# Wide gate and up products, padded values, pair matrices in turn and the inversion first, in a three-network block chain on one core

## The chip, the core and the metric

One Trainium2 chip, one of its cores. The metric is the device time of one execution in microseconds (us). TensorE is called PE here, VectorE DVE, ScalarE ACT, GpSimd POOL and SyncE SP (it issues the DMAs).

## The reference

A first block (layer 1) and a second block of two layers (layer 2, called 0 and 1) work on 256 tokens with 1024 features, and a last norm ends the program. Each layer is a mixer, whose parts are put side by side and projected back to 1024, and a feed-forward network with 2816 hidden units. All in single precision.

```python
# layer 1
h = rms_norm(x, pre_mix_norm)
mix = concat(rg_lru(h), gla_chunked(h), moba_attention(h))   # moba: 8 heads of 64 features
x = x + rms_norm(mix @ w_out, post_mix_norm)
h = rms_norm(x, pre_ffn_norm)
f = (silu(h @ w_ffn_gate) * (h @ w_ffn_up)) @ w_ffn_down
x = x + rms_norm(f, post_ffn_norm)
# layer 2, twice
h = rms_norm_2(x, attn_norm_g)
ya = rwkv7_mixer(...)      # recurrent: 4 heads of 64
yb = dilated_mixer(...)    # attention: 4 heads of 64
yc = mla_mixer(...)        # latent attention: 4 heads, values of 128
x = x + concat(ya, yb, yc) @ w_out
h = rms_norm_2(x, ffn_norm_g)
x = x + (silu(h @ ffn_w_gate) * (h @ ffn_w_up)) @ ffn_w_down

# the recurrent step of rwkv7_mixer
sa = einsum('bhvk,bhk->bhv', state, kk_t)
state = state * w_t - sa[..., None] * b_t + v_t[..., None] * k_t
y = einsum('bhvk,bhk->bhv', state, r_t)
```

## The kernel before

**Split products.** Every weight is read once from HBM as a raw tile of 128 x 1024 (`wraw`, three buffers). ACT rounds it into a high part `whi` (L279), and DVE, for a few POOL (L281, L283), subtracts to get the low part `wlo`. The activations are split likewise: `hT[0]` (tile `hTh`) and `hT[1]` (`hTl`), features on partitions, 256 tokens wide. A product is the sum of three: high by high, high weight by low activation, low weight by high activation. `fm` does that with the weight stationary and the 256 tokens moving (L431 to L433), `tm` with the tokens stationary and 512 weight columns moving (L442 to L445), `mm3` for single pieces (L313 to L315).

**Feed-forward networks** (`ffn`). The 2816 hidden units are 22 blocks of 128; the first two go through `tm`, the other twenty through the loop over f. In it, a block's gate and up products are put side by side into the two halves of one PSUM bank, taken in turn from two pairs, `p` and `r` (48 matmuls 256 wide); ACT takes silu of the gate half (L583), DVE multiplies by the up half (L584), the product `sl` is split into `hd` high and low (ACT L586, DVE L587), and one block later PE multiplies `hd` by the down weights (L313 to L315, twelve matmuls 512 wide) into four banks that stay accumulating.

**Attention** (`attention`, `softmax_head`). For each head: scores into a bank `s`, softmax on DVE and ACT, three transposes of 128 x 128 on PE (L464), and the values' product in two matmuls (L467, L468), which PE does in two passes each as its operands are full single precision. Two heads of 64 features share a bank `o`: one writes its upper 64 rows, the other its lower 64.

**The recurrent mixer** (`recurrent`, generators `c`, `i`, `v`, `o`, `u`) turns the recurrence into blocks of 128 tokens. `pairs` multiplies the decayed keys of one head by `n.AR` (64 features deep, so 64 rows of PE) and copies the masked result from a bank to a zeroed tile: LN in bank `r`, MN in bank `p`, four heads each. `solve` inverts triangular matrices: it starts from the 32 x 32 diagonal blocks, which POOL copies out of LN into `Nd` (L1200), and doubles them in four rounds. A round is a matmul batch `Xd` by LN, a copy `v1` on ACT (L986), a batch `v1` by `Zd` (L976), a masked copy on DVE (L991) and a transpose on DVE (L992, the first one L980); each batch comes in two halves of 16 matmuls 32 x 32. Then the blocks are put together in pairs up to 128 (L1003 and behind).

**Order.** Code is written as generators, and a string (`PLAN1`, `PLAN2`) says in which order their pieces are laid down. A scheduler then orders each engine's instructions by when it takes them to be ready and by priority, which is the order of laying down where nothing else is said. Each engine works in order. PSUM has two banks `p`, two `r`, two `s`, one `t`, one `o`.

## Time and profile before

| | |
|---|---|
| runs | 1023.39, 1024.9 and 1031.35 us, median 1024.9 |
| the profiled execution | 1030.67 us, span 1028.9 us |
| PE busy | 988.9 us (96%) |
| DVE busy | 610.5 us (59%) |
| ACT busy | 515.1 us (50%) |
| POOL busy | 86.2 us (8%) |
| layer 1's mixer | 0 to about 132 us |
| feed-forward, steady | 147 to 324, 497 to 670, 846 to 1021 us |
| layer 2's mixers | about 326 to 476 and 672 to 826 us |

The engines' shares are means over all stages. What a matmul costs in a row of them is read from the distance between the starts, since the duration shown holds the pipeline's tail. "L431" is a line of the kernel before.

### The profile page before, as it was taken

What the parts mean: (1) busy time and instruction counts of PE and PEld (TensorE: products, weight loads), DVE (VectorE), ACT (ScalarE), POOL (GpSimd) and SP (SyncE); (2) the same over time, 40 slices, a digit from 0 to 9 for tenths busy, and PEclk for the clock granted to TensorE, in tenths of its full rate; (3) what the DMA queues carried; (4) which work ended last, traced back from release to release, by engine and by line L of the source; (5) the groups of instructions that cost most, each with busy time, mean ns of one, the idle gap of its engine ahead of it and who ended that gap; (6) DMA issues with size and microseconds to landing.
All of it is one profiled execution on the core that took longest, in us unless ns stands there. A gap on an engine that the chain in (4) does not pass through costs nothing.

```text
span 1028.9 us, 18424 instructions
## 1 busy us (share of the span) xinstructions
PE 988.9 (96%) x7463; PEld 878.2 (85%) x7463; DVE 610.5 (59%) x1098; ACT 515.1 (50%) x890; POOL 86.2 (8%) x117
## 2 busy tenths in 40 slices
PE   5999989999999998999999999999899999999997
PEld 4988769999997977787899999988778879999996
DVE  4777675555667676556555556657852565555653
ACT  5468564444555544355544445546343464444552
POOL 0003100000001144000000000012420000000000
PEclk9999999999999998999999999999996999999999
DMA  7862546555674414105556557543320245555651
GB/s 248 258 188 88 169 155 202 184 187 188 211 237 154 151 52 146 53 27 163 190 194 182 185 189 246 166 144 114 109 82 21 69 140 201 185 185 187 219 168 41
DMA packets 48640, 161.44 MB, mean 157 GB/s; under 512 B 5683, under 2 KB 9004, under 8 KB 48556
## 3 DMA queue, kind: packets, MB, share of 16 engines
q1 hardware_dynamic: 48556, 160.28, 47.5%
q8 instruction: 58, 0.95, 0.4%
q14 instruction: 26, 0.21, 0.1%
HBM read 159.20 MB, written 1.06 MB: 156 GB/s over the span
## 4 chain that ended last, share of the span: by engine, by line
PE 86%; DVE 7%; issue 2%; ACT 2%; POOL 1%; DMA 1%; SPq 0%; POOLq 0%; ACTq 0%; DVEq 0%
PE psp L433 8%; PE psp L431 8%; PE psp L432 8%; PE psr L433 6%; PE psr L432 6%; PE psr L431 6%; PE pss L314 4%; PE pss L315 4%; PE pss L313 4%; PE psp L442 2%; PE psp L445 2%; PE psp L443 2%; PE pst L313 2%; PE pst L315 2%; PE pst L314 2%
## 5 line engine op out<-in xcount | busy, mean ns | idle before, releaser
L281 DVE TENSOR_TENSOR wlo<-wraw,whi 128x1024 fp32r<-128x1024 f32 (+2 forms) x249 | 301.7, 1214 | 241.8 <-ACT whi L279 241.2
L279 ACT ACTIVATE whi<-wraw 128x1024 fp32r<-128x1024 f32 (+3 forms) x266 | 276.0, 1041 | 307.6 <-PE pso L314 63.4
L431 PE MATMUL psp<-hTh,whi 128*128 128x256 f32 x720 | 205.6, 286 | 0.0
L433 PE MATMUL psp<-hTh,wlo 128*128 128x256 f32 x720 | 204.7, 284 | 0.0
L432 PE MATMUL psp<-hTl,whi 128*128 128x256 f32 x720 | 204.5, 284 | 0.0
L431 PEld LDWEIGHTS psp<-hTh,whi 128*128 128x128 f32 x720 | 138.2, 192 | 4.0 <-issue 1.7
L432 PEld LDWEIGHTS psp<-hTl,whi 128*128 128x128 f32 x720 | 138.2, 192 | 1.5 <-issue 0.2
L433 PEld LDWEIGHTS psp<-hTh,wlo 128*128 128x128 f32 x720 | 138.2, 192 | 1.2 <-issue 0.3
L433 PE MATMUL psr<-hTh,wlo 128*128 128x256 f32 x480 | 135.8, 283 | 0.0
L432 PE MATMUL psr<-hTl,whi 128*128 128x256 f32 x480 | 135.8, 283 | 0.0
L431 PE MATMUL psr<-hTh,whi 128*128 128x256 f32 x480 | 135.7, 283 | 0.0
L431 PEld LDWEIGHTS psr<-hTh,whi 128*128 128x128 f32 x480 | 92.0, 192 | 1.2
L432 PEld LDWEIGHTS psr<-hTl,whi 128*128 128x128 f32 x480 | 92.0, 192 | 1.1
L433 PEld LDWEIGHTS psr<-hTh,wlo 128*128 128x128 f32 x480 | 92.0, 192 | 0.0
L367 POOL TENSOR_TENSOR rstd<-msq,neghalf 128x1 f32<-128x1 f32 x18 | 12.3, 681 | 652.0 <-DVE msq L379 652.0
L442 PE MATMUL psp<-whi,hTh 128*128 128x512 f32 (+2 forms) x128 | 48.7, 388 | 5.9 <-ACT hTh L389 5.6
L443 PE MATMUL psp<-wlo,hTh 128*128 128x512 f32 (+2 forms) x128 | 47.4, 378 | 0.0
L283 POOL TENSOR_TENSOR wlo<-wraw,whi 128x1024 fp32r<-128x1024 f32 (+1 forms) x17 | 35.0, 2064 | 41.9 <-ACT whi L279 37.6
L442 PEld LDWEIGHTS psp<-whi,hTh 128*128 128x128 f32 x128 | 24.9, 194 | 12.8 <-ACT hTh L389 7.4
L586 ACT ACTIVATE hd<-sl 128x256 fp32r<-128x256 f32 x60 | 24.4, 407 | 19.9 <-DVE sl L584 19.9
L315 PE MATMUL pss<-wlo,hd 128*128 128x512 f32 x84 | 33.3, 397 | 0.0
L314 PE MATMUL pss<-whi,hd 128*128 128x512 f32 x84 | 33.1, 394 | 0.0
(627 smaller groups left out, 1785.6 us busy)
## 6 DMA issues: line engine op xcount, KB each, us to landing
wraw<-in_ffn_dram SPq DMA_DIRECT2D x198, 512.0 KB, 3.7
wraw<-in_win_dram SPq DMA_DIRECT2D x48, 512.0 KB, 3.8
wraw<-in_wout_dram SPq DMA_DIRECT2D x24, 512.0 KB, 3.6
gain<-in_prow_dram SPq DMA_DIRECT2D x9, 512.0 KB, 4.9
wraw<-in_win_dram SPq DMA_DIRECT2D x8, 480.0 KB, 4.2
wraw<-in_win_dram SPq DMA_DIRECT2D x4, 272.0 KB, 2.8
tb<-bdr SPq DMA_DIRECT2D x4, 256.0 KB, 4.0
wraw<-in_wuq_dram SPq DMA_DIRECT2D x2, 512.0 KB, 3.7
```

What stands on the lines that cost most here:

```text
L279: A.activation(hi, raw, AF.Copy)
L281: V.tensor_sub(lo, raw, hi)
L283: E.tensor_tensor(lo, raw, hi, op=ALU.subtract)
L313: PE.matmul(o, xs[0], ws[0], start=start, stop=False)
L314: PE.matmul(o, xs[1], ws[0], start=False, stop=False)
L315: PE.matmul(o, xs[0], ws[1], start=False, stop=stop)
L431: PE.matmul(o, wh, hT[0][:, k, :], start=(k == 0), stop=False)
L432: PE.matmul(o, wh, hT[1][:, k, :], start=False, stop=False)
L433: PE.matmul(o, wl, hT[0][:, k, :], start=False, stop=(k == KC - 1))
L442: PE.matmul(o, hT[0][:, k, ts], ws[k][0], start=k == 0, stop=False)
L443: PE.matmul(o, hT[0][:, k, ts], ws[k][1], start=False, stop=False)
L586: A.activation(hd[:, 0], sl[:, 1], AF.Copy)
```

## The change

Five parts.

- `inputT` puts high and low activations of one k beside each other, and `fm_wide` multiplies the high weight by both at once: one matmul 512 wide into a whole bank, then the low weight by the high activation, 256 wide, into the bank's second half. The two halves are added afterwards: ACT copies the second half to `cr`, DVE adds the first. Blocks 2 to 20 of each network do this, gate in a bank `p` and up in a bank `r`; the last block stays as it was.
- `padded` gives each 64-feature head a value tile 128 wide with zeros for the other head of its pair, so that both heads' products write all rows of bank `o` and add up. In layer 1 these tiles sit where `AR` and `mna` do.
- `pairs` does two heads at once, into two banks, going back and forth between the upper and the lower 64 rows. Two weight products of 64 rows in the mixer (`pw`, `pa`) go back and forth likewise.
- `solve` does a batch whole, 32 matmuls and one copy of 128 x 256, and its steps get a priority 300 higher.
- The latent attention takes its room from `hTl` first.

```diff
+    def inputT():
+        ts = [big.tile([128, KC // 2, 2, S], F32R, name=n, tag=n) for n in ("hTh", "hTl")]
+        return In(ts, 0), In(ts, 1), ts
+    def fm_wide(wt, hT, o):
+        for k in range(KC):
+            PE.matmul(o, wt[0][:, k], hT[2][k // 4][:, k % 4], start=(k == 0), stop=False)
+            PE.matmul(o[:, S:], wt[1][:, k], hT[0][:, k, :], start=False, stop=(k == KC - 1))
...
+    def padded(t):
+        G.memset(t.rearrange("p (i j) d -> p i (j d)", j=2)[:, :, 64:192], 0.0)
+        v = t.rearrange("p h d -> p (h d)")
+        return bass.AP(tensor=v.tensor, offset=v.offset, ap=[v.ap[0], [256, 2], [192, 2], [1, 64]])
...
-        PE.matmul(o, vs[0], pt[:, :256], start=True, stop=False)
-        PE.matmul(o[:, 128:], vs[1], pt[:, 256:], start=False, stop=True)
+        PE.matmul(o, vs[0], pt[:, :256], start=first, stop=False)
+        PE.matmul(o[:, 128:], vs[1], pt[:, 256:], start=False, stop=last)
...
         for f in range(2, FC):
-            p = bank("pr"[f % 2])
-            for i in range(2):
-                w = weight(ap[3 * f + i])
-                fm([v.rearrange("p (k c) -> p k c", k=KC) for v in w], hT, p[:, i * 256:(i + 1) * 256])
             sl = A2("sl", [128, 2, S])
-            n_.silu = A.activation(sl[:, 0], p[:, :256], AF.Silu)
-            V.tensor_mul(sl[:, 1], sl[:, 0], p[:, 256:])
+            if f < FC - 1:
+                cr = A2("cr", [128, 2, S])
+                for i in range(2):
+                    p = bank("pr"[i])
+                    w = weight(ap[3 * f + i])
+                    fm_wide([v.rearrange("p (k c) -> p k c", k=KC) for v in w], hT, p)
+                    A.activation(cr[:, i], p[:, S:], AF.Copy)
+                    V.tensor_tensor(cr[:, i], p[:, :S], cr[:, i], op=ALU.add)
+                    if i == 0:
+                        n_.silu = A.activation(sl[:, 0], cr[:, 0], AF.Silu)
+                V.tensor_mul(sl[:, 1], sl[:, 0], cr[:, 1])
...
-        mv = [T2(f"mv{t}", [128, 512]) for t in range(2)]
+        mv = [mix.tile([128, 8, 128], F32, name=f"mv{t}", tag=n, bufs=1) for t, n in enumerate(("AR", "mna"))]
+        mv_in = [[padded(v[:, i:i + 4]) for i in (0, 4)] for v in mv]
...
-            for c in range(2):
-                diagonal(c, lambda e, b: nU[e][b, b], lambda e, b: Xd[b, e], p)
-                A.activation(v1[:, hd(c, 4)], all8(p)[:, hd(c, 4)], AF.Copy)
+            diagonal(lambda e, b: nU[e][b, b], lambda e, b: Xd[b, e], p)
+            A.activation(v1, all8(p), AF.Copy)
...
-            yield from solve(n.LN, Nd.rearrange("p c h t -> p (c h) t"), Z, X)
+            steps = solve(n.LN, Nd.rearrange("p c h t -> p (c h) t"), Z, X)
+            while True:
+                with tc.high_priority(300):
+                    if next(steps, steps) is steps:
+                        return
+                yield
...
+        def pairs(src, hp, name, tag):
+            ps, ds = [bank(tag), bank(tag)], []
             for c in range(2):
-                PE.matmul(p[:, hd(c, 256)], src[rs, 2 * hp + c],
-                          n.AR[rs, 2 * hp + c].rearrange("p a t -> p (a t)"), start=True, stop=True)
+                for j in range(2):
+                    PE.matmul(ps[j][:, hd(c, 256)], src[hd(j), 2 * hp + c],
+                              n.AR[hd(j), 2 * hp + c].rearrange("p a t -> p (a t)"), start=True, stop=True)
```

How the order changes, at the places that the prediction speaks of (a row is a run of like instructions; x2 is two of them; the number in front is its place in that engine's list, and line numbers of after are those of the changed kernel).

ACT in a steady block of the first feed-forward network, before:

```order
127 L279 ACTIVATE whi<-wraw 128x1024 x2
128 L583 ACTIVATE sl<-psp 128x256
129 L279 ACTIVATE whi<-wraw 128x1024
130 L586 ACTIVATE hd<-sl 128x256
131 L279 ACTIVATE whi<-wraw 128x1024 x2
```

And after (L293 is the weight copy, L622 the new copy of a half, L625 silu, L635 hd's high part):

```order
131 L622 ACTIVATE cr<-psp 128x256
132 L625 ACTIVATE sl<-cr 128x256
133 L622 ACTIVATE cr<-psr 128x256
134 L293 ACTIVATE whi<-wraw 128x1024
135 L635 ACTIVATE hd<-sl 128x256
136 L293 ACTIVATE whi<-wraw 128x1024 x2
```

Two copies stand between the weight copies and hd; the order of the weight copies is the same.

POOL where the inversion of a mixer begins, before (L1200 is the copy of the diagonal blocks, L283 the low part of a weight):

```order
26 L1216 MEMSET LN 128x512 x4
27 L1200 COPY Nd<-LN 32x2x32 x12
28 L283 TENSOR_TENSOR wlo<-wraw,whi 128x512
29 L1200 COPY Nd<-LN 32x2x32 x4
30 L283 TENSOR_TENSOR wlo<-wraw,whi 128x512 x2
```

And after:

```order
28 L297 TENSOR_TENSOR wlo<-wraw,whi 128x1024
29 L1275 MEMSET LN 128x512 x4
30 L1249 COPY Nd<-LN 32x2x32 x16
31 L297 TENSOR_TENSOR wlo<-wraw,whi 128x512 x3
32 L297 TENSOR_TENSOR wlo<-wraw,whi 128x1024
```

All sixteen copies of the diagonal now come ahead of the three weight differences of 128x512.

PE in the inversion's first round, before (L976 is a batch or half batch; L313 to L315 and L1377 are products of the latent and dilated branches):

```order
2143 L976 MATMUL psr<-Xd,LN 32x32 x16
2144 L1385 MATMUL pss<-dkT,dqT 128x128 x2
2145 L313 MATMUL psp<-whi,ckvh 128x512
2146 L1377 MATMUL pst<-c_83,dq 128x128 x4
2147 L314 MATMUL psp<-whi,ckvl 128x512
2148 L315 MATMUL psp<-wlo,ckvh 128x512
2149 L976 MATMUL psr<-Xd,LN 32x32 x16
2150 L976 MATMUL psr<-Zd,v_4165 32x32 x25
```

And after (L1026 is a batch, L468 to L471 the mixer's input product):

```order
1829 L1026 MATMUL psr<-Xd,LN 32x32 x32
1830 L469 MATMUL psp<-wlo,hTl 128x512
1831 L468 MATMUL psp<-whi,hTl 128x512
1832 L469 MATMUL psp<-wlo,hTl 128x512
1833 L1026 MATMUL psr<-Zd,v_3982 32x32 x32
1834 L471 MATMUL psp<-whi,hTl 128x512 x4
1835 L327 MATMUL psp<-whi,cqh 128x256
1836 L328 MATMUL psp<-whi,cql 128x256
1837 L1026 MATMUL psr<-Xd,LN 32x32 x32
```

The first batch now stands inside the input product, and the second round begins eight rows later. In before's list, the first batches of the four rounds are rows 2143, 2208, 2219 and 2248; in after's they are rows 1829, 1837, 1849 and 1860.

## Rows read from the trace of the kernel before

**Rows 1.** The page: busy time of each engine; the chain that ended last

```profile
PE 988.9 (96%) x7463; PEld 878.2 (85%) x7463; DVE 610.5 (59%) x1098; ACT 515.1 (50%) x890; POOL 86.2 (8%) x117
...
PE 86%; DVE 7%; issue 2%; ACT 2%; POOL 1%; DMA 1%; SPq 0%; POOLq 0%; ACTq 0%; DVEq 0%
```

**Rows 2.** Windows (start:end, length, busy us by engine, PEclk, DMA share, GB/s)

```profile
147.00:324.00 177.00, 176.96 (x1229) 164.71 (x1228) 99.25 (x122) 85.64 (x125) 0.55 (x1) 1.00 0.58 195
...
346.00:476.00 130.00, 123.34 (x1309) 104.16 (x1309) 81.91 (x210) 62.27 (x135) 27.39 (x37) 0.97 0.30 95
...
690.00:826.00 136.00, 130.16 (x1311) 109.65 (x1310) 82.11 (x209) 62.41 (x135) 27.45 (x37) 0.92 0.27 87
...
773.00:793.50 20.50, 20.50 (x125) 17.48 (x122) 5.06 (x13) 5.00 (x11) 0.00 (x0) 0.50 0.08 24
```

**Rows 3.** Timeline (start us, us) of PE, two heads' value products

```profile
417.56 0.65 PE L467 MATMUL pso<-pt,dv 128*64 128x256 f32 x2
...
418.35 1.05 PE L1254 MATMUL psp<-c,r__3885 128*128 128x2 f32 x8
...
452.45 0.60 PE L467 MATMUL pso<-pt,hTl 128*128 128x256 f32 x2
...
453.11 0.38 PE L464 MATMUL pst<-c,sc 128*128 128x128 f32 x2
```

**Rows 4.** Timeline of PE, pair matrices, and two groups of the second mixer

```profile
376.29 1.14 PE L1219 MATMUL psr<-AR,be 64*128 64x256 f32 x8 [1.46 <-DVE be L1186]
...
419.33 1.13 PE L1219 MATMUL psp<-AR,ka 64*128 64x256 f32 x4
...
759.84 1.13 PE L1219 MATMUL psp<-AR,ka 64*128 64x256 f32 x4
...
802.12 0.60 PE L467 MATMUL pso<-pt,hTl 128*128 128x256 f32 x2
```

**Rows 5.** Timeline of PE, a steady block of the first feed-forward network

```profile
244.14 0.39 PE L313 MATMUL pss<-whi,hd 128*128 128x512 f32 x1
...
246.91 0.28 PE L431 MATMUL psr<-hTh,whi 128*128 128x256 f32 x1
247.03 0.28 PE L432 MATMUL psr<-hTl,whi 128*128 128x256 f32 x1
```

**Rows 6.** Timeline of all engines, start of the first mixer's inversion

```profile
383.74 0.39 PE L442 MATMUL psp<-whi,hTh 128*128 128x512 f32 x1
383.79 1.46 POOL L283 TENSOR_TENSOR wlo<-wraw,whi 128x512 fp32r<-128x512 f32 x1 [1.12 <-issue]
...
385.10 1.08 PE L445 MATMUL psp<-whi,hTl 128*128 128x512 f32 x4
385.19 1.04 POOL L1200 COPY Nd<-LN 32x64 f32<-32x64 f32 x4
...
386.61 1.23 DVE L1189 TENSOR_SCALAR ok<-pcol 128x2 f32<-128x2 f32 x1
387.76 0.43 DVE L980 STREAM_TRANSPOSE Xd<-Zd 128x256 f32<-128x256 f32 x1
...
388.33 0.45 PE L976 MATMUL psr<-Xd,LN 32*32 32x32 f32 x32 [1.44 <-DVE Xd L980]
```

**Rows 7.** Groups, 147 to 324 us (count, busy us, mean ns, idle before)

```profile
L281 DVE TENSOR_TENSOR wlo<-wraw,whi 128x1024 fp32r<-128x1024 f32 x56 | 68.5, 1225 | 68.7 <-ACT whi L279 68.7
L279 ACT ACTIVATE whi<-wraw 128x1024 fp32r<-128x1024 f32 x56 | 59.2, 1059 | 75.8 <-issue 18.3 <-PE pso L314 18.2 <-PE psp L432 12.6
...
L584 DVE TENSOR_TENSOR sl<-sl,psr 128x256 f32<-128x256 f32 x10 | 4.2, 416 | 0.1
...
L583 ACT ACTIVATE sl<-psr 128x256 f32<-128x256 f32 x10 | 3.7, 367 | 0.9 <-PE psr L433 0.9
```

**Rows 8.** PE's waits from 370 to 410 us (us in total, times, longest)

```profile
PE pst L1410 <- DVE hTl L1412: 1.5, 1, 1.5
...
PE psr L1219 <- DVE LN L1221: 0.6, 1, 0.6
```

More of the change, by code (lines that the diff above doesn't have):

```diff
@@ L69, with __init__, __getitem__ @@
 WB = (3, 5)
+class In:
+    def __init__(self, ts, j):
+        self.ts, self.j = ts, j
+    def __getitem__(self, at):
+        p, k, c = at
+        if isinstance(k, slice):
+            t = k.start // 4
+            return self.ts[t][p, k.start - 4 * t:k.stop - 4 * t, self.j, c]
+        return self.ts[k // 4][p, k % 4, self.j, c]
 class Names:
@@ L577, in ffn @@
         for f in range(2, FC):
-            p = bank("pr"[f % 2])
-            for i in range(2):
-                w = weight(ap[3 * f + i])
-                fm([v.rearrange("p (k c) -> p k c", k=KC) for v in w], hT, p[:, i * 256:(i + 1) * 256])
             sl = A2("sl", [128, 2, S])
-            n_.silu = A.activation(sl[:, 0], p[:, :256], AF.Silu)
-            V.tensor_mul(sl[:, 1], sl[:, 0], p[:, 256:])
+            if f < FC - 1:
[9 more added lines that the diff above has]
+                V.tensor_mul(sl[:, 1], sl[:, 0], cr[:, 1])
+            else:
+                p = bank("p")
+                for i in range(2):
+                    w = weight(ap[3 * f + i])
+                    fm([v.rearrange("p (k c) -> p k c", k=KC) for v in w], hT, p[:, i * 256:(i + 1) * 256])
+                n_.silu = A.activation(sl[:, 0], p[:, :256], AF.Silu)
+                V.tensor_mul(sl[:, 1], sl[:, 0], p[:, 256:])
             hd = A2("hd", [128, 2, S], F32R)
@@ L971, in solve, with diagonal @@
         V.tensor_copy(Zd, C("eye").unsqueeze(1).to_broadcast([128, 8, 32]))
-        def diagonal(c, lhs, rhs, p):
-            for e in range(4 * c, 4 * c + 4):
+        def diagonal(lhs, rhs, p):
+            for e in range(8):
                 for b in blocks:
@@ L1039, in latent_in @@
             wv += [[v.rearrange("p (k c) -> p k c", k=2) for v in w] for w in zip(his, los)]
-        dv = A2("dv", [128, 2, 256])
+        dv = [A2("dv", [128, 4, 128]) for _ in range(2)]
+        dv_in = [padded(v) for v in dv]
         qT = (A2("cqh", [128, 2, S], F32R), A2("cql", [128, 2, S], F32R))
@@ L1133, in inverses @@
                 PE.matmul(pw[:, hd(c, 256)], dec[0:64, hd(c, 128)], xx[0:64, 0], start=True, stop=True)
-            for c in range(2):
                 PE.matmul(pa[:, hd(c, 256)], dec[64:128, hd(c, 128)], xx[64:128, 0], start=True, stop=True)
@@ L1195, in inverses @@
             n.LN, Nd = [], T1("Nd", [128, 2, 4, 32])
-            for h in range(4):
-                n.LN.append(pairs(n.be, h, "LN", "r"))
-                for b in range(4):
-                    bs = hd(b, 32)
-                    G.tensor_copy(Nd[bs, :, h], n.LN[h][bs, :, 0, bs])
-                if h % 2:
-                    yield
+            for hp in range(2):
+                n.LN += pairs(n.be, hp, "LN", "r")
+                for h in (2 * hp, 2 * hp + 1):
+                    for b in range(4):
+                        bs = hd(b, 32)
+                        G.tensor_copy(Nd[bs, :, h], n.LN[h][bs, :, 0, bs])
+                yield
             Z = mix.tile([128, 8, 128], F32, name="Z", tag="Z", bufs=1)
@@ L1386, in score @@
             PE.matmul(p[:, 128:384], q[:, 128:], k, start=True, stop=True)
[L1388 removed]
+        yield from attention(score, lambda h: C("dil"), 0.125, lambda h: (dv[0][:, h], dv[1][:, h]), 0, 4, 64, mixT, 2)
     def latent(l, mixT, cq, ckv, krT):
@@ L1393, in latent @@
         wk = [weight(a[f"wkv_{l}"][:, hd(i, 512)], G) for i in range(2)]
-        room = [big.tile([128, 4, 512], F32, name=n, tag=n) for n in ("hTh", "hTl")]
+        room = [big.tile([128, 4, 512], F32, name=n, tag=n) for n in ("hTl", "hTh")]
         room = [v[:, i] for v in room for i in range(4)]
```

52 lines of the change are left out of this document (25 added, 27 removed).

## The prediction

> **What bounds the kernel now.** I read the page's engine totals and its chain of waits first. TensorE (PE) is busy 988.9 of 1028.9 us, and 86% of the chain that ended last is PE [rows 1]. So what counts is PE's own time, plus the places where it waits. The windows by stage say where those are [rows 2]: in the first feed-forward stretch (147 to 324 us) PE is busy 176.96 of 177.00 us, so time there changes only if PE's instructions get shorter, or if something new is late. In the two recurrent mixers (346 to 476 and 690 to 826 us) PE idles 6.7 and 5.8 us, and the granted clock is 0.97 and 0.92. Behind the 0.92 stand 20.5 us granted at 0.50, the lower of the clock's two levels [rows 2].
>
> **The base.** The profiled execution took 1030.67 us, 1.8 us above its span, and 5.8 above the median of the runs shown. The low clock explains that much: both mixers run the same program, and the distance between like matmuls of the two grows from 340.5 us (419.33 to 759.84) to 349.7 us (452.45 to 802.12) [rows 3, 4], so the late stretch at half clock cost 9.2 us. Runs of 1023.4 and 1024.9 can't hold it. I take the typical run as the base: 1030.7 - 5.8 = 1024.9.
>
> **Gate and up products.** In the steady part of a feed-forward network, matmuls 256 columns wide start 0.12 us apart, and 512-wide ones farther apart: twelve of the down product fill 244.14 to 246.91 us, 0.231 us each [rows 5]; in the mixer's input product, six steps of alternating 512-wide ones go from 383.74 to 385.10, 0.227 us each [rows 6]. Of each k step before, 3 x 0.120 = 0.360 us; after it is one 512-wide and one 256-wide. With 0.227 that is 0.347, with 0.231 it is 0.351. The change does this for 19 blocks of 128 hidden units, two products, 8 k steps and three networks: 912 steps. That gives 912 x 0.013 = 11.9 us or 912 x 0.009 = 8.2 us. Those down products also change their moving operand's tile and their bank as they go. The new pair holds on to one bank and one weight tile at a time, like the input product, so I take 0.228: **-11.0 us**. Bounds: 0.240 (two 256-wide ones, no gain) and 0.227 (-11.9).
>
> The row says a matmul costs 13 ns beyond its columns (two of 256 cost 0.240, one of 512 0.227). The Trainium skill, "TensorE: Matmul & The Clock Gate", section "Back-to-back issue gap", gives N/2.4 + 2.5 ns for one matmul at full clock, thus only about 2.5 ns saved for each pair that is merged. By that page the term would be 912 x 2.5 ns = 2.3 us and the whole forecast some 9 us longer; it stands below as a rival. The rows here do not fit it (0.120 us for 256 columns, where its formula makes 0.109).
>
> What this costs elsewhere: for each block, two copies 128x256 out of PSUM on ACT (0.37 us each, as the silu from PSUM takes) and two adds on DVE (0.42 us each, as the product with PSUM) [rows 7]. Over 57 blocks that is 42 us of ACT and 47 us of DVE. A block's period is 48 x 0.12 + 2.77 = 8.5 us [rows 5], and in it ACT has three weight copies (1.06 us each) and DVE three weight differences (1.23 us each), besides short ones [rows 7]. So ACT comes to about 3 x 1.06 + 4 x 0.38 = 4.7 us and DVE to 3 x 1.23 + 4 x 0.42 = 5.4 us of 8.3. Neither fills. Next the chain: from the end of a gate product (0), ACT first converts the weight that waits for the same matmul (to 1.1), copies the half (1.4); DVE does the weight difference (2.4), the add (2.8); silu ends at 3.2. The up product ends at 2.8, its copy at 3.5, its add at 4.0, the multiply at 4.4, hd's high part at 4.9, one more weight difference on DVE (5.8), hd's low part at 6.1. PE wants hd after up, the down product of the block before, and the next gate and up: 4 x 2.77 = 11.1. About **5 us of slack**, so I cost the additions at nothing. The cover is that slack. Weights come in the same order, one period ahead, and DVE frees the raw buffers with the difference that still stands ahead of the adds. PSUM: a block now takes one bank of each of two pairs, where before it took one; each is used again two blocks later, 16 us, so nothing waits.
>
> **Padded values.** A head of 64 features writes 64 PSUM rows: its four matmul passes take 0.79 us (417.56 to 418.35). A head of 128 takes 0.66 (452.45 to 453.11) [rows 3]. With padding the first becomes like the second: 0.13 us less for 8 heads of MoBA and 2 x 4 dilated ones, 16 x 0.14 = **-2.2 us** (I add 0.01 for the entry into a half array; bounds 0 and -3). The zeroing is a few memsets on POOL, which is busy for a fifth of a mixer [rows 2]. In layer 1 the values sit in the two tiles that later hold out-projection weights, so these must wait for the last head; in the new order they are needed 25 matmuls of 512 columns after that, 5.7 us, and a conversion takes 1.06 + 1.23. Nothing.
>
> **Pair matrices.** One head of MN takes 1.06 us of 64-row passes alone (x4, 419.33, and the duration shown has the last pass's tail). Two LN heads that happened to alternate between row halves took the same 1.07 for eight passes (x8, 376.29; 1.14 with its tail) [rows 4]. So two heads in turn cost one. Four MN heads in each mixer: two times 1.06 saved, in two mixers 4.2 us. The second LN group, already half overlapped, gives perhaps 0.3 each. **-4.5 us** (bounds -2.5, if the new waits below eat part, and -5). The new wait: both banks of p hold MN, and the projection behind it needs one back, after a 0.7 us copy on DVE; three rows of other work lie between. The two weight products of decay and rate already ran together, so interleaving them is worth 0.
>
> **Inversion whole and first.** Before, the first round started late: POOL's last copies of the diagonal (385.19) stood behind a weight difference of 1.46 us (383.79), then DVE's transpose (387.76) behind a 1.23 us operation (386.61), and PE waited 1.44 us until 388.33 [rows 6]. LN's bank cost 0.6 us, and a rotation in the latent branch 1.5 us more [rows 8]. After, POOL's copies stand ahead of that difference, and copy and transpose come first on DVE. That saves about 1.2 us in each mixer. On the other side, the eight half rounds of the diagonal, spread over 40 us before, stand close: in each a matmul batch of 0.5 us, then either a 0.4 us ACT copy with 0.35 of latency around it, or two DVE steps (0.43 each, as the transpose of [rows 6]) with 0.45 around them. Between two batches PE has 0.5 to 1.4 us of other matmuls in the new order, against 0.75 and 1.3 needed: about 1 us of waiting a mixer if nothing is queued on ACT and DVE. Those work in order: a weight copy of 1.06 us [rows 7] in front of a third of them makes it 2.7. Net per mixer -1.2 + 2.7 = +1.5, for both **+3 us** (bounds -4, where these waits and the latent one go, and +8, each half round behind one weight copy that its filler half hides). The rest of the mixer has less filler, but PE is full there with attention and projections, and ACT and DVE are busy half and two thirds of the mixer [rows 2].
>
> **Sum:** 1024.9 - 11.0 - 2.2 - 4.5 + 3 = 1010.2; forecast **1010 us**, which is 20.7 under the profiled execution, 5.8 of them the clock.
>
> **Rivals.**
> *The wide matmul gives little.* The spacing of 512 columns that also fill a bank might be 0.233 to 0.240. For it: the down product shows 0.231. Against it: the input product, at 0.227 with weight tiles alternating as well. At 0.2375 the term is -2.3, and the time 1019 us. Chance 0.12.
> *Solve first turns into waits and low clock.* The clock fell to 0.50 before, among the solve's batches and waits, and the long stretch cost 9.2 us. If one mixer gets it in the typical run, 1019 us; with the +8 bound as well, 1024. For it: 32x32 batches packed with waits between them. Against: half of that pattern was there before, and the median run didn't have the long stretch. Chance 0.20.
> *The late hd (slower).* In the feed-forward networks hd, now behind two copies and two adds, reaches PE late. It decides only from 5 us of additional delay in the chain above. With 0.5 us of wait in each block, 57 x 0.5 = 28.5: 1039 us. It could come if ACT's weight copies, in order ahead of the new ones, waited for a late transfer; PE's 176.96 of 177.00 us [rows 2] shows no such lateness now. Chance 0.05.
> *The change doesn't do what it says*: PE's list falls from 5539 rows to 4632, so the merge is there. No chance of its own.
>
> **How the numbers follow.** Main case 0.63, 1003 to 1016 by its bounds; the first rival 1015 to 1021, the second 1015 to 1024. The range 1002 to 1022 leaves out the top of the second, the slow one, and luck on the good side (all waits gone: 1001). A measurement can tell about 1% here, 10 us: faster means under 1014.7, slower over 1035.1. Of the main case I put 0.03 above 1014.7; the first rival is all within 1%, of the second a quarter lies below. Faster 0.65, same 0.30, slower 0.05.
>
> **What would show it.** In the profile after: 512-wide gate matmuls followed 0.22 to 0.23 us later by a 256-wide one, the three networks still without idle PE and shorter by 3 to 4 us each; ACT at some 55 to 57% and DVE at 63 to 65% there; PV of every head near 0.66 us; MN as two groups of eight passes near 1.07 us; the inversion's rounds within about 25 us, PE's waits on its copies and transposes under 4 us a mixer. It would be wrong if the wide matmul needs 0.235 or more, if PE waits for hd, or if the mixers grow by over 5 us each.

## The result and the profile after

The changed kernel took 1015.05 us (median of four runs, 1014.5 to 1016.77) where the kernel before, on the same chip, took 1024.14 (median of four, 1023.19 to 1031.35). The ratio is 0.9899 with a 95% interval of 0.9852 to 0.9946: 9.1 us faster, against 14.9 forecast from the median (1010 from 1024.9). The time lies in the forecast range. Medians here are over all runs; the ratios leave out runs that were visibly disturbed.

The page of the profile after (span 1013.2 us; busy time of each engine, and the chain that ended last) stands against [rows 1]:

```profile
PE 966.9 (95%) x6551; PEld 820.6 (81%) x6551; DVE 654.3 (65%) x1212; ACT 548.4 (54%) x995; POOL 87.5 (9%) x125
...
PE 81%; DVE 8%; DMA 4%; ACT 3%; issue 2%; POOL 1%; SPq 0%; POOLq 0%; ACTq 0%; DVEq 0%
```

PE lost 22 us of busy time, DVE gained 44 and ACT 33: the halves' copies and adds. PE's share of the last chain fell from 86 to 81%: there is a little more waiting than before. The windows (start and end, length, busy us of each engine, granted clock, DMA share, GB/s) of the first network, the two mixers and the last network, as [rows 2]:

```profile
147.00:324.00 177.00, 175.78 (x928) 149.15 (x927) 113.36 (x159) 97.75 (x162) 1.18 (x3) 1.00 0.64 193
...
346.00:476.00 130.00, 124.27 (x1326) 105.68 (x1326) 83.97 (x215) 64.35 (x137) 27.24 (x37) 0.97 0.33 100
...
690.00:820.00 130.00, 122.66 (x1313) 103.70 (x1312) 85.19 (x214) 65.56 (x136) 27.11 (x37) 0.99 0.30 91
847.00:1005.00 158.00, 158.00 (x840) 134.82 (x839) 98.28 (x143) 83.13 (x140) 0.55 (x1) 1.00 0.59 174
```

The last network is still without idle PE. In the first one PE now idles 1.2 us, where it idled 0.04. The second mixer's window has a clock of 0.99 where it had 0.92.

Where the 15.6 us between the two profiled executions are follows from the same events in both traces (first and last down product of a network):

| stretch | before | after | difference |
|---|---|---|---|
| start to network 0's first down product | 167.40 | 168.48 | +1.1 |
| network 0, first to last down product | 159.06 | 158.67 | -0.4 |
| mixer 0 | 186.40 | 182.98 | -3.4 |
| network 1 | 159.07 | 158.61 | -0.5 |
| mixer 1 | 190.85 | 180.43 | -10.4 |
| network 2 | 159.02 | 157.02 | -2.0 |

Of mixer 1's 10.4 us, the long stretch at half clock that only the execution before had is about 9. Without it mixer 1 is some 1.2 us shorter. By the sum (+1.5 for the inversion, -2.25 for pairs, -0.55 for padding) each mixer should have been 1.3 shorter, so the mixers did no worse than forecast. It is the networks that should have brought 11 us and brought 3.

**The wide products** work as planned. Timeline of PE in a steady block (start, duration shown), as [rows 5]:

```profile
238.32 0.39 PE L458 MATMUL psp<-hTh,whi 128*128 128x512 f32 x1
238.54 0.28 PE L459 MATMUL psp<-hTh,wlo 128*128 128x256 f32 x1
238.66 0.40 PE L458 MATMUL psp<-hTh,whi 128*128 128x512 f32 x1
...
243.96 0.39 PE L327 MATMUL pss<-whi,hd 128*128 128x512 f32 x1
```

One 512-wide and one 256-wide matmul take 0.34 us in the first step (238.32 to 238.66), and the whole pair of products 5.64 us (to 243.96), where it was 48 x 0.12 = 5.76. Over the 255 steps between 180 and 310 us the means are 0.2333 + 0.1169 = 0.350 us. Two rows give the period of a block, the first down product and the one fourteen blocks later:

```profile
168.48 0.39 PE L327 MATMUL pss<-whi,hd 128*128 128x512 f32 x1
...
285.84 0.39 PE L327 MATMUL pss<-mixTh,hd 128*128 128x512 f32 x1
```

(285.84 - 168.48) / 14 = 8.38 us, where it was 8.53. Nineteen blocks in three networks at 0.143 us are 8.2 us. But networks 0 and 1 kept only 0.4 and 0.5 of their 2.7 us. Their ends show why. Timeline at the end of network 0, rows of DVE, ACT and PE (in brackets the idle time ahead and what ended it):

```profile
312.09 0.43 DVE L626 TENSOR_TENSOR sl<-sl,cr 128x256 f32<-128x256 f32 x1
...
313.16 0.63 ACT L305 ACTIVATE wv<-wraw 128x512 fp32r<-128x512 f32 x1 [2.36 <-DMA wraw<-in_win_dram]
...
313.70 0.40 ACT L635 ACTIVATE hd<-sl 128x256 fp32r<-128x256 f32 x1
...
314.44 0.42 DVE L636 TENSOR_TENSOR hd<-sl,hd 128x256 fp32r<-128x256 f32 x1
...
314.91 0.50 PE L328 MATMUL pss<-dl,hd 128*128 128x512 f32 x1 [0.25 <-DVE hd L636]
...
317.07 0.42 ACT L635 ACTIVATE hd<-sl 128x256 fp32r<-128x256 f32 x1 [0.97 <-DVE sl L633]
...
317.54 0.50 PE L327 MATMUL pss<-dl,hd 128*128 128x512 f32 x1 [0.97 <-ACT hd L635]
```

DVE had block 20's product ready at 312.5 (`sl`, 312.09 + 0.43). ACT was not free for hd's high part: in its order stands a weight of the next mixer (`wv`), and it waited 2.36 us for that weight's transfer. So hd's high part started at 313.70, its low part at 314.44, and PE waited 0.25 us for it until 314.91; then the last block's silu and hd stood behind two more weight copies, and PE waited 0.97 us until 317.54. Counted from start to start, where such matmuls otherwise lie 0.23 us apart, the two waits and the slower matmuls behind them cost 2.0 us. In the kernel before, hd of block 20 came ahead of `wv`. Timeline of ACT there:

```profile
310.88 0.42 ACT L586 ACTIVATE hd<-sl 128x256 fp32r<-128x256 f32 x1 [1.29 <-DVE sl L584]
312.58 1.15 ACT L291 ACTIVATE wv<-wraw 128x512 fp32r<-128x512 f32 x2 [1.28 <-DMA wraw<-in_win_dram]
```

Network 2 has no mixer behind it, and no such wait.

**The pair matrices.** Timeline of PE in the second mixer, MN, as [rows 4]:

```profile
764.20 1.13 PE L1271 MATMUL psp<-AR,ka 64*128 64x256 f32 x8
...
769.95 1.13 PE L1271 MATMUL psp<-AR,ka 64*128 64x256 f32 x4
771.01 1.14 PE L1074 MATMUL psr<-Z,v 64*64 64x64 f32 x16
772.08 1.13 PE L1271 MATMUL psp<-AR,ka 64*128 64x256 f32 x4
```

The first two heads run in turn: eight passes in 1.06 us. The second two don't: the order put a batch of the inversion (L1074) between them, and each head takes its 1.06 us alone, as before.

**The inversion.** PE's waits in the first mixer, 370 to 470 us (total, times, longest):

```profile
PE psr L1026 <- issue: 1.8, 1, 1.8
PE psr L1271 <- DVE be L1234: 1.5, 1, 1.5
PE psr L1026 <- DVE Xd L1030: 0.9, 1, 0.9
PE psr L1271 <- DVE LN L1276: 0.6, 1, 0.6
```

Together 4.8 us around the pairs and the inversion, 2.7 of them on the inversion's own batches (L1026), where they were 1.4 [rows 6]. The inversion's diagonal rounds and first joins ran from 386.06 to 406.48 us, where they ran from 388.33 to 432.02.

### The profile page after: what moved, and what is told of

Read it like the earlier page. It is cut to its first block, busy times and chain, and to the rows that moved or that the text cites. A ratio compares the mean times of both kernels' runs of the same rounds, so it can differ in the third digit from the quotient of the medians.

```text
span 1013.2 us, 16837 instructions
## 1 busy us (share of the span) xinstructions
PE 966.9 (95%) x6551; PEld 820.6 (81%) x6551; DVE 654.3 (65%) x1212; ACT 548.4 (54%) x995; POOL 87.5 (9%) x125
## 3 DMA queue, kind: packets, MB, share of 16 engines
HBM read 159.20 MB, written 1.06 MB: 158 GB/s over the span
## 4 chain that ended last, share of the span: by engine, by line
PE 81%; DVE 8%; DMA 4%; ACT 3%; issue 2%; POOL 1%; SPq 0%; POOLq 0%; ACTq 0%; DVEq 0%
PE psr L458 10%; PE psp L458 10%; PE psp L459 5%; PE psr L459 5%; PE pss L328 3%; PE pss L329 3%; PE pss L327 3%; DMA wraw<-in_win_dram 3%; PE psp L445 3%; PE psp L446 3%; PE psp L447 3%; PE psp L468 2%; PE psp L469 2%; PE psp L471 2%; PE pst L327 2%
## 5 line engine op out<-in xcount | busy, mean ns | idle before, releaser
L293 ACT ACTIVATE whi<-wraw 128x1024 fp32r<-128x1024 f32 (+3 forms) x266 | 275.9, 1040 | 236.6 <-PE psp L458 69.2
L458 PE MATMUL psp<-hTh,whi 128*128 128x512 f32 x228 | 82.8, 396 | 0.0
L458 PE MATMUL psr<-hTh,whi 128*128 128x512 f32 x228 | 82.5, 396 | 0.0
L458 PE MATMUL psp<-hTl,whi 128*128 128x512 f32 x228 | 82.5, 395 | 0.0
L458 PE MATMUL psr<-hTl,whi 128*128 128x512 f32 x228 | 82.4, 395 | 0.0
L459 PE MATMUL psp<-hTh,wlo 128*128 128x256 f32 x228 | 64.1, 281 | 0.0
L625 ACT ACTIVATE sl<-cr 128x256 f32<-128x256 f32 x57 | 23.8, 417 | 57.8 <-DVE cr L623 57.8
L458 PEld LDWEIGHTS psr<-hTl,whi 128*128 128x128 f32 x228 | 42.8, 188 | 10.2
L458 PEld LDWEIGHTS psp<-hTl,whi 128*128 128x128 f32 x228 | 42.7, 187 | 10.1
L458 PEld LDWEIGHTS psp<-hTh,whi 128*128 128x128 f32 x228 | 42.8, 188 | 9.8
L459 PEld LDWEIGHTS psp<-hTh,wlo 128*128 128x128 f32 x228 | 43.0, 189 | 3.1 <-DVE wlo L295 0.7
L445 PE MATMUL psp<-hTh,whi 128*128 128x256 f32 x144 | 42.0, 292 | 0.0
L446 PE MATMUL psp<-hTl,whi 128*128 128x256 f32 x144 | 41.6, 289 | 0.0
```

Source lines behind the costliest of these rows:

```text
L293: A.activation(hi, raw, AF.Copy)
L445: PE.matmul(o, wh, hT[0][:, k, :], start=(k == 0), stop=False)
L446: PE.matmul(o, wh, hT[1][:, k, :], start=False, stop=False)
L458: PE.matmul(o, wt[0][:, k], hT[2][k // 4][:, k % 4], start=(k == 0), stop=False)
L459: PE.matmul(o[:, S:], wt[1][:, k], hT[0][:, k, :], start=False, stop=(k == KC - 1))
L625: n_.silu = A.activation(sl[:, 0], cr[:, 0], AF.Silu)
```

## Experiments

Runs of one kernel differ here by some 25 us, and nearly all of it is the granted clock (the share of full speed that the chip grants TensorE; a stretch lies either at 0.50 or at 1.00, and a run's mean between them): over 65 runs of the kernel before (1019.42 to 1044.97 us, mean clock 0.971 to 0.998) a straight line through time and mean clock has a slope of 951 us per unit of clock and a correlation of 0.98, and reaches 1016.3 us at full clock. So two numbers are given for each kernel besides its median: the mean clock (median over its runs), and the time at full clock, an estimate: the mean over its runs of time less 951 us x (1 - clock), with the slope of the kernel before taken for all. Its spread from run to run is 1 to 2 us (0.4 in the first four runs of the changed kernel), so differences of under 2 us between kernels of four or five runs say little. The last column is the time at half clock inside the two mixers in the profiled execution.

| kernel | median us | ratio to before (95%) | clock | at full clock | half clock in mixers |
|---|---|---|---|---|---|
| before, three sets of runs | 1028.35, 1031.69, 1032.24 | | 0.989, 0.984, 0.983 | 1016.4, 1016.5, 1016.0 | 27.3 |
| changed (the result above) | 1015.05 | 0.9899 (0.9852 to 0.9946) | 0.9925 | 1008.2 | 10.2 |
| e5 changed, again | 1013.97 | 0.9817 (0.9775 to 0.9859) | 0.9955 | 1008.1 | 3.4 |
| e1 wide only | 1043.24 | 1.0129 (1.0073 to 1.0185) | 0.969 | 1012.6 | 75.0 |
| e2 no wide | 1023.75 | 0.9948 (0.9909 to 0.9988) | 0.993 | 1016.4 | 10.2 |
| e3 old tail | 1018.17 | 0.9924 (0.9887 to 0.9960) | 0.994 | 1011.8 | 3.4 |
| e4 no priority | 1031.73 | 1.0036 (1.0005 to 1.0067) | 0.9805 | 1012.6 | 40.9 |
| e6 wide, room | 1022.82 | 0.9925 (0.9878 to 0.9972) | 0.9875 | 1011.1 | 13.6 |
| e7 inversion first only | 1030.72 | 1.0003 (0.9963 to 1.0042) | 0.9925 | 1022.2 | 10.2 |
| e8 first, halves | 1014.41 | 0.9823 (0.9779 to 0.9866) | 0.995 | 1009.1 | 3.4 |
| e9 not first, halves | 1031.75 | 1.0030 (0.9987 to 1.0074) | 0.978 | 1010.6 | 41.0 |
| e10 old pairs | 1019.85 | 0.9936 (0.9892 to 0.9980) | 0.991 | 1011.7 | 3.4 |
| e11 ends | 1010.35 | 0.9828 (0.9761 to 0.9895) | 0.995 | 1005.5 | 3.4 |
| e12 ends, DVE | 1010.23 | 0.9834 (0.9760 to 0.9908) | 0.994 | 1004.1 | 3.4 |

e1 to e4, e5 to e8 and e9 to e12 each ran on one chip, together with one of the three sets of the kernel before, to which their ratios refer.

**e1, the wide products alone**, in the kernel before.

```diff
-                fm([...], hT, p[:, i * 256:(i + 1) * 256])
+                    fm_wide([...], hT, p)
+                    A.activation(cr[:, i], p[:, S:], AF.Copy)
+                    V.tensor_tensor(cr[:, i], p[:, :S], cr[:, i], op=ALU.add)
```

> The kernel before with the wide gate and up products alone (blocks 2 to 20 of each network, with their copies and adds). Theory E (the ends): a k step costs 0.233 + 0.117 = 0.350 us in place of 0.360, so a block's period falls by 0.14 us, 2.7 us in each network, 8.2 in all; at the end of networks 0 and 1 PE waits for the last hd, because ACT does a weight copy of the next mixer first and that waits for its transfer, 1.7 us each: some 4.7 us faster than before, 1019.4 us, and PE's waits on hd only at those two ends. Rival F (the forecast's term): 11 us faster, 1013. Rival C (ACT and DVE in all blocks eat the gain): no block's period under 8.5 us, 1024.

All three missed: 1.3% slower than before. The networks were near theory E's figures: network 2 got 2.1 us shorter between its first and last down product, network 0 only 0.5, with 1.2 us of waits on hd at its end; at network 1's end there was no wait, and it got 2.3 us shorter. But with the new layout of the activations the tile `hTl` is no longer the low part, it is the last four k steps, and the latent branch's room is taken there first unless the change's fifth part is made too. PE's wait for that (total, times, longest):

```profile
PE pst L1448 <- DVE hTl L1450: 8.1, 2, 4.1
```

Two waits of 4.1 us, and the clock then fell in both mixers, 75 us at half clock in all. It is a flaw of the experiment, but together with e6 it shows what the swap of the room's order is for.

**e6, the same with the room's order swapped.**

```diff
-        room = [big.tile([128, 4, 512], F32, name=n, tag=n) for n in ("hTh", "hTl")]
+        room = [big.tile([128, 4, 512], F32, name=n, tag=n) for n in ("hTl", "hTh")]
```

> The kernel before with the wide products and, with them, the latent branch's room taken from the low tile's place first, as in the changed kernel; the earlier wide-only kernel lacked that and PE waited 4.1 us twice for a rotation. Theory H: those two waits go (8 us), the inversion is still spread, so the clock stays as in the kernel before or somewhat lower: 2 to 8 us under the kernel before, 18 us or more under the earlier wide-only kernel. Rival (the wide networks themselves lower the clock): as slow as the earlier wide-only kernel, 1.3% over the kernel before.

Theory H held: 20 us under e1, 0.7% under before, the clock as before (0.9875). At full clock the wide products alone are worth 5.2 us.

**e2, all but the wide products.**

```diff
-            if f < FC - 1:
-                cr = A2("cr", [128, 2, S])
-                ...
+            p = bank("pr"[f % 2])
+            for i in range(2):
+                w = weight(ap[3 * f + i])
+                fm([...], hT, p[:, i * 256:(i + 1) * 256])
```

> The changed kernel with the old gate and up products (256 wide, no copies and adds); padded values, pairs in turn and inversion first stay. Theory E: the networks are back at 8.53 us a block with no wait at their ends, so 4.7 us slower than the changed kernel, 1019.7. Rival F: 11 us slower, 1026. Rival C: same as the changed kernel, 1015.

At full clock 1016.4, no better than before: in the presence of the other parts the wide products are worth 8.2 us, which is all that the change gains there. That lies between theory E and rival F, and rival C is out. Not all of it was found in the networks: in e2's trace the three take 4.4 and 5.3 us longer, first to last down product, than in the two executions of the changed kernel; where the rest lies is open. Nor are e2's networks free of the waits: in network 0 PE waits 0.2 and 0.5 us for hd, so old products alone don't keep hd early.

**e3, the old products in the last three blocks.**

```diff
-            if f < FC - 1:
+            if f < FC - 3:
...
-                p = bank("p")
+                p = bank("pr"[(f + 1) % 2])
```

> The changed kernel with the old products in the last three blocks of each network, not in the last one alone, so that hd of these blocks is made before ACT turns to the next mixer's weights. Theory E: the waits on hd at the ends of networks 0 and 1 go (3.4 us), two more old blocks in each network cost 6 x 0.14 = 0.9: 2.5 us faster than the changed kernel, 1012.5. Rival (the wait at the end has another cause, as a late down weight): it stays, and the time is 1016.

In its trace the waits on hd at the ends are smaller, not gone (0.47 us in network 0, 0.08 in network 1), and networks 0 and 1 took 158.01 and 157.21 us between their first and last down product, 0.7 and 1.4 us less than in the changed kernel's. The time missed theory E: 1018.17 us, 1011.8 at full clock, 3.5 over the changed kernel where 2.5 under it were expected. In the trace its mixers are the slower part; why is open. e11 mends the ends without giving up blocks.

**e4, whole batches without the priority.**

```diff
-            while True:
-                with tc.high_priority(300):
-                    if next(steps, steps) is steps:
-                        return
-                yield
+            yield from steps
```

> The changed kernel without the higher priority of the inversion's steps (whole batches stay). By the forecast's term the inversion first costs 1.5 us in each mixer, so this kernel is 3 us faster than the changed one, 1012. Theory G (from the two traces: the mixers came out 3.4 and about 2.5 us shorter, of which pairs and padding explain 2.8 each): order alone is worth under 1 us in each mixer, 1014 to 1017. Rival (the first rounds' late start was what mattered): 3 us slower, 1018, with PE waiting for the first transpose again.

All expectations were too small: 1031.73 us, some 17 over the changed kernel, most of it clock (0.9805, 40.9 us at half clock in the mixers). This is what made the clock the question.

**e5, the changed kernel again.** No edit.

> The changed kernel once more, beside the others of this call. Theory H (the clock): what the change moves most is how long the clock is granted at 0.50 in the two mixers; here 7 to 17 us at half clock in all, mean clock 0.991 to 0.994, 9 to 12 us under the kernel before. Rival E (the sum of PE's own times alone, the clock alike in both): the distance to the kernel before is 8 us whatever their clocks.

17.7 us under the kernel before on this chip, where before had a clock of 0.984; 9.1 in the result above. At full clock it is 8.4 here. Theory H was right about the clock, with a difference larger than it said; rival E is right about what remains when the clock is taken out.

This second trace also shows that the waits on hd change from one execution to the next. In network 1 PE waited only 0.25 us at the end, and network 0 had one at 294 us, well ahead of its end. Timeline of ACT and PE there:

```profile
291.50 1.06 ACT L293 ACTIVATE whi<-wraw 128x1024 fp32r<-128x1024 f32 x1 [1.58 <-DMA wraw<-in_ffn_dram]
292.46 0.40 ACT L635 ACTIVATE hd<-sl 128x256 fp32r<-128x256 f32 x1
...
294.21 0.50 PE L328 MATMUL pss<-mixTh,hd 128*128 128x512 f32 x1 [0.79 <-DVE hd L636]
```

A weight copy ahead of hd in ACT's order waited 1.58 us for its transfer, and PE then 0.79 us for hd.

**e7, the inversion whole and first in the kernel before.**

```diff
+            diagonal(lambda e, b: nU[e][b, b], lambda e, b: Xd[b, e], p)
+            A.activation(v1, all8(p), AF.Copy)
...
+                with tc.high_priority(300):
+                    if next(steps, steps) is steps:
+                        return
```

> The kernel before with the inversion's batches whole and its steps first, and nothing else of the change. Theory H: the half-clock time in the two mixers falls to some 7 us, mean clock about 0.993, and this part alone is worth 4 to 8 us. Rival (the forecast's term): it costs 3 us. Rival (pairs in turn are needed with it): the clock stays at 0.985 to 0.990 and the time within 2 us of before.

No theory alone: the clock rose to 0.9925, and the time at full clock rose by 5.9 us, so the median is where it was. In its trace PE waits 4.9 us for the inversion's batches in the first mixer, where it was 1.4 before. The forecast's +3 was of the right sign for this part taken alone.

**e8, first, but in halves.** The changed kernel with the old `diagonal(c, ...)`.

```diff
-            diagonal(lambda e, b: nU[e][b, b], lambda e, b: Xd[b, e], p)
-            A.activation(v1, all8(p), AF.Copy)
+            for c in range(2):
+                diagonal(c, lambda e, b: nU[e][b, b], lambda e, b: Xd[b, e], p)
+                A.activation(v1[:, hd(c, 4)], all8(p)[:, hd(c, 4)], AF.Copy)
```

> The changed kernel with the inversion's batches in halves again, still first. Theory H with the order as its cause: like the changed kernel within 2 us, clock 0.991 to 0.994. Rival (whole batches are the cause): like the kernel without the priority, 12 to 16 us over the changed one, clock near 0.98.

As the changed kernel, in time (medians 0.4 us apart, 1.0 at full clock) and clock. The order matters, the size of the batches doesn't.

**e9, in halves and not first.** Both edits of e4 and e8: wide products, padding and pairs in turn are what is left of the change.

> The changed kernel with the inversion as it was, in halves and not first; wide products, padded values and pairs in turn stay. Theory I (order and pairs hang together): the spread inversion brings the half clock back as in the kernel that had whole batches without priority (mean clock 0.980 to 0.987), 8 to 16 us over the changed kernel. Rival (only whole batches without priority were bad): clock 0.990 or more and within 3 us of the changed kernel.

Theory I: 0.978, 1031.75 us, no faster than before. Its windows (the granted clock is the third number from the right):

```profile
432.20:449.30 17.10, 17.10 (x105) 14.87 (x106) 3.71 (x9) 4.18 (x8) 0.00 (x0) 0.50 0.07 19
449.30:469.00 19.70, 19.25 (x128) 16.12 (x128) 12.37 (x51) 10.41 (x35) 2.02 (x2) 1.00 0.05 19
780.40:797.50 17.10, 17.10 (x107) 14.78 (x106) 4.43 (x14) 5.48 (x14) 0.00 (x0) 0.50 0.10 32
```

17.1 us at 0.50 in each mixer, PE busy all the time. The first of them begins among the inversion's last joins and the second MN pair. Timeline of PE there, one row a group:

```profile
428.58 0.69 PE L1053 MATMUL psr<-Xd,LN 32*32 32x32 f32 x16
429.20 0.70 PE L1269 MATMUL psp<-AR,ka 64*128 64x256 f32 x4
...
430.77 1.10 PE L1321 MATMUL psp<-vc,MN 128*128 128x64 f32 x8
...
432.10 1.87 PE L1321 MATMUL psp<-vc,MN 128*128 128x64 f32 x8
...
434.90 0.90 PE L497 MATMUL pst<-c,sc 128*128 128x128 f32 x3
```

32x32 joins (L1053, L1059), 64-row MN passes (L1269) and 64-wide products (L1321) follow each other; the clock falls at 432.2. In the changed kernel the 32x32 joins are over at 408.5, and the same part of the mixer goes

```profile
408.00:442.00 34.00, 33.63 (x265) 28.85 (x262) 17.96 (x50) 16.37 (x37) 10.25 (x9) 0.95 0.25 73
442.00:460.00 18.00, 17.67 (x112) 14.52 (x110) 11.71 (x45) 8.95 (x28) 2.02 (x2) 1.00 0.09 33
747.00:781.00 34.00, 33.62 (x278) 28.85 (x276) 18.37 (x52) 17.26 (x38) 10.24 (x9) 1.00 0.24 68
```

with one short fall (0.95 of the window) in the first mixer and none in the second.

**e10, pairs one head after the other.**

```diff
-                MN = pairs(n.ka, hp, "MN", "p")
...
                 for hh in range(2):
                     h = 2 * hp + hh
+                    MN = pairs(n.ka, h, "MN", "p")
```

> The changed kernel with the pair matrices of one head after the other, as before. In the trace after, only one MN group of each mixer runs as eight passes in 1.06 us; the other is cut in two by a batch of the inversion and costs 1.06 + 1.06 as before. Theory J: pairs in turn save 1.06 us in each mixer and little else, so this kernel is 2 to 3 us slower than the changed one. Forecast's term: 4.5 us slower. Theory I as well (inversion first needs pairs in turn): 6 us slower or more, the waits of the inversion back at 5 us a mixer.

At full clock 3.5 us over the changed kernel, the medians 5 to 6 apart (across chips). That lies between theory J and the forecast's term, and the spread doesn't tell them apart; nor do the traces, where the two mixers together take 2.8 or 5.0 us longer than in the two executions of the changed kernel, if half of the time at half clock is taken off. Theory I's 6 or more isn't reached.

**e11, the ends mended.** ACT converts the value weights of the next mixer after the network's last hd.

```diff
-            A.activation(hd[:, 0], sl[:, 1], AF.Copy)
+            n_.hd = A.activation(hd[:, 0], sl[:, 1], AF.Copy)
...
-            weight_to(W.words(i), his, los)
+            with behind([n_.hd]):
+                weight_to(W.words(i), his, los)
```

> The changed kernel with the two value weights of the next mixer converted behind the last hd of a network, in ACT's order. Theory E: PE's waits on hd at the ends of networks 0 and 1 go, 1.5 us at each end in the trace; in the time 2 to 3 us less if the weights are not missed later. Rival: these weights, now later, are waited for in the mixer's head, and the time stays.

ACT at the end of network 0:

```profile
313.14 0.42 ACT L635 ACTIVATE hd<-sl 128x256 fp32r<-128x256 f32 x1 [1.81 <-DVE sl L626]
...
316.10 0.42 ACT L635 ACTIVATE hd<-sl 128x256 fp32r<-128x256 f32 x1 [0.17 <-DVE sl L633]
...
316.58 1.14 ACT L305 ACTIVATE wv<-wraw 128x512 fp32r<-128x512 f32 x2
```

hd of the last two blocks now comes ahead of `wv`, and PE waits for neither. Networks 0 and 1 took 156.68 and 156.70 us, 2.0 and 1.9 less than in the changed kernel's first trace, 2.4 and 0.7 less than in its second (e5). 1010.35 us, 2.7 us less at full clock. Theory E is shown.

**e12, and DVE in POOL's place in layer 1.**

```diff
-                w = halves_of(weight(ap[k], G if i < 3 else None))
+                w = halves_of(weight(ap[k], G if i < 3 and not room else None))
```

> The same, and the first three out-projection weights of layer 1 get their low part from DVE, not from POOL. In the trace after, DVE's scaling of sc in layer 1 takes 2.01 us where it otherwise takes 0.29, and ends 0.08 us after POOL's weight difference beside it. Theory K (DVE waits for POOL there): that operation is back at 0.3 us, PE's 2.4 us of waiting for sc at 94 to 100 us goes, 2 us faster than the kernel with mended ends. Rival: DVE's own three differences of 1.2 us, now in its row, make PE wait as long.

The operation in question, in the changed kernel and in this one (shortest, median and longest ns of its 24 executions):

```profile
L493 DVE TENSOR_SCALAR sc<-sc,rc x24: 244/286/2012, 59.6 to 795.2; 128x128 f32<-128x128 f32 x24
```

```profile
L493 DVE TENSOR_SCALAR sc<-sc,rc x24: 244/286/290, 60.7 to 790.5; 128x128 f32<-128x128 f32 x24
```

The long one is gone, and so is PE's wait for it. The stretch up to network 0's first down product, half of its time at half clock taken off, is 165.9 us where e11's is 167.7, as theory K says. The median is the same as e11's (1010.23), 1.4 us less at full clock, which is within the spread. Both are the fastest versions here, 1.7% under the kernel before on their chip, and 3.6 to 4.8 us under the changed kernel across chips.

## Why the prediction came out as it did

The measured time lies in the forecast's range and on its side, 5 us above the figure; the gain was 9.1 us in place of 14.9. The sum's terms, 14.7 us, stand against 8.2 at full clock. The wide products' size (2.8 us) and the waits on hd (3.9 us in the first trace, 3.1 in e5's, by e11's networks) are as large as that difference. That the other errors nearly cancel is luck: an inversion that took 2.5 us off, where the sum added 3, stands against 4.5 us of waits in layer 1 that the sum doesn't have; and nothing in the sum foresaw the clock. By its steps:

- **Base.** The 5.8 us between the profiled execution and the median were put down to the long stretch at half clock. That fits the runs since, and is far too narrow a reading: the clock is not a matter of one run, it differs with how a mixer is ordered. The second rival ("solve first turns into waits and low clock") had the sign of the clock wrong; the waits came where the part stands alone (e7). With the inversion spread the median clock is 0.969 to 0.989 (before, e1, e4, e6, e9), with it first 0.991 to 0.9955. In e4 and e9 the mixers have 41 us at half clock (e6's one trace, at a clock of 0.990, has 13.6); no trace of the eight kernels whose inversion is first has more than 10.2, and none a stretch over 6.8 there.
- **Gate and up products, -11.0.** The step gained 0.0094 us, not 0.012: 0.350 in place of the 0.348 taken, 8.2 to 8.6 us in the steady blocks. By the rule of the Trainium skill quoted there, it would have been 2.3; the trace speaks against it.
- **"About 5 us of slack, so I cost the additions at nothing."** Failed at two of three ends. The slack was counted in a steady block, whose weights were taken to come one period ahead. At the end of a network ACT's next conversion belongs to the next mixer and waits for its transfer, ahead of hd. The slow rival named just that, a weight copy in order ahead of the new copies that waits for a late transfer, and took the kernel before as a sign that it doesn't come; e5 has such a wait well ahead of an end too. Price, by e11's networks without the waits: 2.0 and 1.9 us in the first trace, 2.4 and 0.7 in e5's.
- **Padded values, -2.2.** The passes of a 64-feature head fell from 0.79 us to between 0.64 and 0.76 where nothing came between. The mean is 0.69, so some 0.10 us a head, 1.6 in all: the 0.66 read in [rows 3] was the low end of the 128-wide heads, which took 0.66 to 0.76, and no row shows the 0.01 us added for the entry into a half array. The stretch up to network 0 still came out 1.1 us longer. It has 3.4 us of half clock at 143.7, and PE's waits in it grew from 15.1 to 19.7 us, by 1.9 us in the first 20 us, where PE waits 1.7 us for a weight's high part (L293), and by 2.1 at 94 to 100 us, where DVE's scaling of the scores waited for POOL (below; 2.4 us against 0.2 before). Padding by itself was not run.
- **Pair matrices, -4.5.** 3.5 by e10, within the spread. Only half of the MN pairs run in turn; that a batch stands between the other two is in the order of the changed kernel and was passed over.
- **Inversion, +3.** As a part added alone it costs 5.9 us at full clock (e7). In the changed kernel it takes 2.5 us off (1008.1 against e9's 1010.6; 4.5 against e4, without the priority alone), and the clock is 0.9925 and 0.9955 in place of 0.978: the medians lie 17 to 18 us apart. PE's waits on its batches came about as summed (2.7 us in the first mixer, 1.4 before). What the order saves elsewhere was left to the bound of -4: the latent branch's waits (L1410), 2.6 us in the first mixer before, are gone in the changed kernel, and in e7 too, where only the inversion was changed. So the parts don't add: removed one at a time from the changed kernel, wide products, pairs and order cost 8.2, 3.5 and 2.5 us at full clock, 14.2 together, while all of it gains 8.2.

That the order of the inversion moves the clock is shown by e4, e8 and e9. What made the clock fall is shown only in part. The fourteen traces have 34 stretches of 3.4 us at half clock ahead of the program's end. 29 of them begin within 2.2 us after PE had stood idle for 0.9 to 4.3 us. The other five (423.6 us in the changed kernel, 760.6 in e5, and the like in e8, e11 and e12) have no idle time of 0.5 us in the 8 us ahead of them, and neither have the nine long ones (10 us and more; before at 773.0, e9 at 432.2 and 780.4, e4 at 437.1 and 781.9, four in e1). The long ones begin where small matmuls stand close, those of the inversion and of attention, in seven of the nine with 64-row pairs, and PE is busy all through. The Trainium skill, "TensorE: Matmul & The Clock Gate", section "HAM oscillation — how this bites in real kernels", tells of idle PE as the cause; that fits the 29, and no row here shows it for the other fourteen.

Nor are those small matmuls enough by themselves. In the kernel before, the 8 us ahead of 773.0 hold the same matmuls in the same numbers as the 8 us ahead of 432.5 in the first mixer, and there the clock did not fall (window of that trace, as [rows 2]):

```profile
425.00:445.00 20.00, 19.90 (x239) 16.80 (x227) 9.95 (x26) 10.70 (x26) 0.00 (x0) 1.00 0.15 39
```

What decides between the two was not tried, and stays open.

## What to carry to other kernels

A slack counted in a loop's steady part says nothing of its ends: look at the last two rounds separately, where an engine's next instruction in order may belong to the next stage and wait for a transfer. Look at a second execution too, since a wait for a transfer differs between them. When the bound engine's clock can fall, compare mean clock and time together, over many runs, before a part of a change is credited: here the inversion first was worth 1 us in the median in the kernel before (e7) and 17 in the changed one (e9). Parts of a change that move the same order have to be undone one at a time from the finished kernel, as they don't add up.

## What the runs showed of the hardware

**DVE waits for POOL.** Timeline of POOL, DVE and PE in layer 1 of the changed kernel:

```profile
93.71 2.36 POOL L297 TENSOR_TENSOR wlo<-wraw,whi 128x1024 fp32r<-128x1024 f32 x1 [4.45 <-ACT whi L293]
...
94.14 2.01 DVE L493 TENSOR_SCALAR sc<-sc,rc 128x128 f32<-128x128 f32 x1
...
96.02 0.74 POOL L798 TENSOR_TENSOR vg<-vg,rp 128x256 f32<-128x256 f32 x1
96.08 0.83 DVE L494 TENSOR_SCALAR sc<-sc,rc 128x256 f32<-128x256 f32 x1
96.21 0.33 PE L497 MATMUL pst<-c,sc 128*128 128x128 f32 x1 [1.34 <-DVE sc L493]
```

DVE's scaling of 128x128, 0.29 us elsewhere, took 2.01 us and ended at 96.15, 0.08 us after POOL's 2.36 us weight difference (96.07); the next one took 0.83 and ended at 96.91, after POOL's next (96.76). PE, which wanted the result, waited 1.34 us. With that POOL work on DVE (e12) all 24 take 0.24 to 0.29; the 128x256 one beside POOL's `vg` still takes 0.85. The kernel before had such a wait too, 0.97 us at 95.9, which cost PE 0.2. The Trainium skill, "SBUF — State Buffer", section "🔬 SBUF: two separate sides", says that DVE and POOL share a pair of ports that one instruction holds to its end; the trace agrees. Not every DVE operation was held up beside such a POOL instruction: one that reads PSUM (`vg`, 93.81 us) took its 0.42, and a reduction of `go` at 97.17 us its 0.40.

**Wide matmuls** took 0.233 us for 512 columns in this stream, whether ACT and DVE were busy beside them or not (between 180 and 310 us 0.2331 us with only ACT busy, 0.2333 with only DVE, 0.2332 with both and 0.2336 with neither), and the 256-wide ones between them 0.117 where they take 0.120 among their like.
